# Two branches' first scores in one product, and sums of squares taken by ScalarE's accumulator

## The chip, the cores and the metric

The kernel runs on one core of one Trainium2 chip. The metric is the device time of one execution in microseconds, as the median of several runs: 623.28 us for the kernel before (three runs, 620.89 to 623.8). The engines are named as the profile names them: PE is TensorE (PEld its weight loads), DVE VectorE, ACT ScalarE, POOL GpSimd, SP SyncE.

## The reference, cut to what matters

The kernel computes a decoder trunk of two layers on 512 tokens of width 1024. Layer 0 has an mLSTM half and an attention half of 8 query heads in 2 groups, 64 wide. Attention has three branches; two of them, the selected blocks and the sliding window, come out here as plain causal attention, each with keys and values of its own.

```python
qh = partial_rope(rms_norm(heads(q, NSA_HEADS), q_norm), pos) * (d ** -0.5)
ks_h = partial_rope(rms_norm(heads(ks, G), k_norm[1]), pos)      # branch 0 in the kernel
kw_h = partial_rope(rms_norm(heads(kw, G), k_norm[2]), pos)      # branch 1
...
p_s = masked_softmax(s_s, tok_ok[:, :, None])
o_s = jnp.einsum('bgrqn,bgqnd->bgrqd', p_s, vs_g)
...
s_w = jnp.einsum('bgrqd,bgnd->bgrqn', q_blk, kwb)
...
return g_blk[..., 0:1] * o_c + g_blk[..., 1:2] * o_s + g_blk[..., 2:3] * o_w
```

`rms_norm` divides by the root of the mean square over the 64 elements of a head, so each q and k needs one sum of squares for every token and head: 8 for q, 4 for k (2 branches of 2 groups). Layer 1 is a gated linear recurrence, which the change leaves alone.

## The kernel before

All matrices of layer 0 are taken in groups of 512 columns (`Group`, `dense0`): cg, nq, nkv, nz, mq, mk, mv, mo, mz and the output projection. Each 512-column product exists three times, since weights and activations are split into a high and a low part in fp32r (`whi`, `wlo`, `h0h`, `h0l`). ScalarE makes `whi` and VectorE makes `wlo` from the loaded weights (`cvt_w`, L738), one group ahead.

Attention runs beside these products as strands of its own. For each of the four chunks of 128 tokens, `prep_q` (L1210) squares the 8 heads in one ScalarE instruction into a big buffer `sq`, lets GpSimd multiply q in place by the norm's weights, lets VectorE reduce `sq` to `qss`, lets GpSimd form the inverse root (`rsqrt_mean`, L710: a multiply-add and a power), and then VectorE scales (`x2`) and rotates. TensorE turns the result and ScalarE and VectorE drain it into high and low parts (`q2`). `prep_k` (L1239) does the same for the 4 key heads into `kd`. Both start when two of the five big buffers (`hb`, `b_t`, tag `big`) are free.

`nsa_a` (L1307) then goes through 16 units: 2 groups, 2 pairs, 2 branches, 2 halves (`UN`, L1303). For each of a unit's four chunks i it makes scores against keys up to that chunk, n = 128 (i + 1) columns, in two products (c = 0, 1) into a PSUM bank `sc` of which there are two. VectorE adds the mask and takes the row extreme (`nm`), ScalarE takes the exponential with its row sum (`sm`), and after the four chunks VectorE scales them by gate over sum. `nsa_b` turns the probabilities (`tp`), copies them (`PT`) and multiplies them with the values (`ac`).

The order of instructions on each engine isn't that of the source. `Flow` emits all operations of a layer under estimated times, and `Plan.flush` (L392) then lists them anew over the whole layer: `schedule` (L284) gives each engine its next operation by estimated start and latest due time, in six rounds of which the best is kept. The estimates for ScalarE and VectorE come from `price` (L517). For ScalarE it is this line, in which `scal` counts inputs of one column, an accumulator output among them:

```python
return low + (55 if psum else 93) + 95 * scal + (88 if "accum_out" in k else 0) + 0.833 * n - (95 if "accum_out" in k else 0)
```

So the engines run in a fixed order, each waiting for its next instruction only. All operations pass through one helper, so the profile gives L408 for nearly all of them; they are told apart by the tiles they write and read (out<-in).

Of the kernel before, what the change touches and what calls it, by code (L numbers as in the profile page):

```python
# [17 lines left out]
OP = mybir.AluOpType  # L18
# [597 lines left out]
def build(tc, I, out):  # L616
# [6 lines left out]
    with ExitStack() as ctx:  # L623
# [323 lines left out]
        with ExitStack() as c0:  # L947
# [261 lines left out]

            def prep_q(i):  # L1210
                yield hb(2)
                x = qk[i][:, :8, :]
                ts_ = slice(128 * i, 128 * (i + 1))
                sq = b_t("sq", (8, 64))
                A.activation(sq, x, AF.Square)
                P.tensor_tensor(x, x, cust(qnB, [[0, 8], [1, 64]]), op=OP.mult)
                ss = s_t("qss", [128, 8])
                V.tensor_reduce(ss, sq, axis=AX.X, op=OP.add)
                b_end()
                rq = s_t("qrs", [128, 8])  # L1220
                rsqrt_mean(rq, ss, 8, 1.0 / 64)
                x2 = b_t("x2", (8, 64))
                V.tensor_tensor(x2, x, cust(rq, [[1, 8], [0, 64]]), op=OP.mult)
                rot(x2, i)
                yield [None, TPS, (lambda: q2) if i else has(2)]
                if i == 0:
                    q2.extend(u_t("q2", (2, 2, 512), F32R) for _ in range(2))
                p4 = turn(x2)
                b_end()
                for o in range(2):  # L1230
                    a, b = slice(64 * o, 64 * o + 64), slice(64 - 64 * o, 128 - 64 * o)
                    for g in range(2):
                        pg = p4[a, 2 * g:2 * g + 2]
                        A.activation(q2[g][a, o, :, ts_], pg, AF.Copy)
                        V.tensor_tensor(q2[g][b, o, :, ts_], pg, q2[g][a, o, :, ts_].bitcast(F32), op=OP.subtract)
                fl.mark(E("q%d" % i))
                fl.add(cmp_sm(i), 2)

            def prep_k(i):  # L1239
                yield hb(2)  # L1240
                x = qk[i][:, 8:, :]
                ts_ = slice(128 * i, 128 * (i + 1))
                sq = b_t("sq", (4, 64))
                A.activation(sq, x, AF.Square)
                P.tensor_tensor(x.rearrange("p (a b) c -> p a b c", a=2), x.rearrange("p (a b) c -> p a b c", a=2),
                                cust(knB, [[64, 2], [0, 2], [1, 64]], 64), op=OP.mult)
                ss = s_t("kss4", [128, 4])
                V.tensor_reduce(ss, sq, axis=AX.X, op=OP.add)
                b_end()
# [57 lines left out]
            def nsa_a():  # L1307
                yield [E("q%d" % i) for i in range(4)] + [E("k%d" % i) for i in range(4)] + [E("gt")]
                for u, (g, pr, br, hh) in enumerate(UN):
# [3 lines left out]
                    nm = s_t("nm", [128, 4], 3)  # L1313
                    sm = s_t("sm", [128, 4], 3)
                    for i in range(NT):
# [3 lines left out]
                        for c in range(2):  # L1319
                            T.matmul(s[:, :n], q2[g][:, hh, pr, 128 * i:128 * (i + 1)], kd[g][:, c, br, :n],  # L1320
                                     start=c == 0, stop=c == 1)
                        V.tensor_tensor_reduce(s[:, :n], s[:, :n], cz[:, 512 - n:], 1.0, -NEG, op0=OP.add, op1=OP.min,
                                               accum_out=nm[:, i:i + 1])
                        A.activation(pp[:, OFF[i]:OFF[i] + n], s[:, :n], AF.Exp, bias=nm[:, i:i + 1], scale=-1.0,
                                     accum_out=sm[:, i:i + 1])
                    V.reciprocal(sm, sm)
                    V.tensor_tensor(sm, sm, cust(gt, [[24, 4]], 3 * hg + 1 + br), op=OP.mult)
                    for i in range(NT):
                        sl = slice(OFF[i], OFF[i] + 128 * (i + 1))
                        V.tensor_scalar(pp[:, sl], pp[:, sl], sm[:, i:i + 1], None, op0=OP.mult)  # L1330
                    PPs[u] = pp
# [6 lines left out]
            def nsa_b():  # L1338
                pts = []
                yp = None  # L1340
                for u, (g, pr, br, hh) in enumerate(UN):
                    yield [E("A%d" % u), hb(1)]
                    pp = PPs.pop(u)
                    ptl = b_t("PT", (1280,))
                    m = []
                    for kbs, o in (((0,), 0), ((1,), 512), ((2, 3), 896)):
# [3 lines left out]
                        for kb in kbs:  # L1350
                            for i in range(kb, NT):
                                T.transpose(tp[:, c:c + 128], pp[:, OFF[i] + 128 * kb:OFF[i] + 128 * (kb + 1)], idf)
# [766 lines left out]
```

## Time and profile before

| | |
|---|---|
| median of 3 runs | 623.28 us (620.89 to 623.8) |
| the profiled execution | 619.54 us |
| its span, first to last instruction | 617.8 us |
| mean granted clock of TensorE | 0.997 |
| TensorE busy | 609.2 us, 4498 products |
| VectorE busy | 463.9 us |
| ScalarE busy | 326.4 us |
| GpSimd busy | 104.5 us |

Rows of the trace all come from the one profiled execution. Its own time is 1.74 us over its span. Preparation of q and k lies at about 36 to 104 us of the span, the 16 units of attention at 104 to 235 us, the mLSTM heads and the output projection up to about 347 us, and layer 1 after that. A product's printed duration is longer than its distance to the next one, because products are pipelined and their ends are modelled; the distance between starts is what a product costs TensorE.

### The profile page before, as it was taken

The numbers are of one execution on the slowest core, as the hardware profiler recorded it, in microseconds if no ns is written. First come the engines' busy times: TensorE is split into PE (matmuls) and PEld (weight loads), VectorE is DVE, ScalarE is ACT, GpSimd is POOL, SyncE is SP. The second block draws the span as 40 slices with busy tenths as digits, with TensorE's granted clock in tenths as the row PEclk, the third lists the DMA queues.
The fourth block names the chain that finished last, engine by engine and source line by source line (L and its number), as shares of the span: only waits on it lengthen the run. The fifth ranks groups of instructions, "written<-read, shape, count | busy, mean of one in ns | idle before, by whom it ended". The sixth has DMA issues, their size and how long they took to land.

```text
span 617.8 us, 11670 instructions
## 1 busy us (share of the span) xinstructions
PE 609.2 (99%) x4498; PEld 492.0 (80%) x4498; DVE 463.9 (75%) x988; ACT 326.4 (53%) x778; POOL 104.5 (17%) x131
## 2 busy tenths in 40 slices
PE   8999998999999999999999999999999999999997
PEld 8877886877777777888888887788877877788886
DVE  5888989988899875656746669997688798986441
ACT  7554433675676765273534757447527375565410
POOL 1424252031100000063003111023000100122100
PEclk9998999999999999999999999999999999999999
DMA  8823137679994004016244424473222215473111
GB/s 293 278 117 103 51 103 256 203 164 342 247 203 138 0 2 147 7 46 228 77 162 136 154 85 138 118 240 121 69 72 69 70 34 173 138 282 128 35 69 68
DMA packets 23526, 82.90 MB, mean 134 GB/s; under 512 B 3376, under 2 KB 4272, under 8 KB 20656
## 3 DMA queue, kind: packets, MB, share of 16 engines
q1 hardware_dynamic: 21168, 65.39, 32.2%
q0 software_dynamic: 2304, 16.78, 10.3%
q8 instruction: 35, 0.57, 0.4%
q14 instruction: 19, 0.16, 0.1%
HBM read 77.96 MB, written 20.97 MB: 160 GB/s over the span
## 4 chain that ended last, share of the span: by engine, by line
PE 92%; DVE 3%; DMA 1%; issue 1%; POOL 1%; ACT 1%; SPq 0%; ACTq 0%; DVEq 0%
PE mm L408 35%; PE mx L408 17%; PE my L408 15%; PE sc L408 8%; PE tp L408 5%; PE ac L408 5%; PE tq L408 5%; PE sd L408 2%; DMA raw<-in_wall_dram 1%; DVE wlo L408 1%; DVE HB L408 0%; DVE AL L408 0%; POOL krs L408 0%; ACT whi L408 0%; DVE x L408 0%
## 5 line engine op out<-in xcount | busy, mean ns | idle before, releaser
L408 ACT ACTIVATE whi<-raw 128x512 fp32r<-128x512 f32 (+1 forms) x184 | 105.0, 614 | 76.2 <-PE my L408 29.5
L408 DVE TENSOR_TENSOR wlo<-raw,whi 128x1024 fp32r<-128x1024 f32 (+1 forms) x96 | 114.7, 1202 | 20.4 <-ACT whi L408 20.1
L408 PE MATMUL mm<-whi,h0h 128*128 128x512 f32 (+1 forms) x168 | 68.2, 407 | 0.0
L408 PE MATMUL mm<-whi,h0l 128*128 128x512 f32 (+1 forms) x168 | 67.9, 405 | 0.0
L408 PE MATMUL mm<-wlo,h0h 128*128 128x512 f32 (+1 forms) x168 | 67.4, 405 | 0.0
L408 ACT ACTIVATE PP<-sc,nm 128x128 f32<-128x128 f32 (+2 forms) x64 | 33.7, 527 | 26.0 <-DVE nm L408 22.9
L408 DVE CUSTOM_DVE_ANT_0 sc<-sc,cz 128x128 f32<-128x128 f32 (+2 forms) x64 | 31.4, 502 | 11.7 <-PE sc L408 9.1
L408 PE MATMUL mm<-h0h,whi 128*128 128x512 f32 x96 | 39.5, 411 | 0.0
L408 PE MATMUL mm<-h0h,wlo 128*128 128x512 f32 x96 | 38.1, 397 | 0.6 <-DVE wlo L408 0.6
L408 PE MATMUL mm<-h0l,whi 128*128 128x512 f32 x96 | 38.6, 402 | 0.0
L408 PEld LDWEIGHTS mm<-whi,h0l 128*128 128x128 f32 x168 | 32.1, 192 | 5.8 <-issue 0.2
L408 PEld LDWEIGHTS mm<-wlo,h0h 128*128 128x128 f32 x168 | 32.2, 192 | 5.6 <-issue 0.2
L408 PEld LDWEIGHTS mm<-whi,h0h 128*128 128x128 f32 x168 | 32.3, 192 | 5.2
L408 DVE TENSOR_TENSOR HB<-HB,tt 128x512 f32<-128x512 f32 x48 | 31.9, 687 | 4.4 <-PE sd L408 3.1
L408 PE MATMUL sc<-kd,q 128*128 128x512 f32 (+3 forms) x128 | 31.3, 330 | 0.0
L408 ACT ACTIVATE PT<-tp 128x384 f32<-128x384 f32 (+1 forms) x48 | 24.0, 526 | 9.5 <-PE tp L408 9.2
L408 POOL TENSOR_TENSOR ivgg<-ivgg,zz 128x256 f32<-128x256 f32 x16 | 17.8, 1116 | 65.9 <-ACT zz L408 65.9
L408 POOL TENSOR_SCALAR hr<-hs 128x4 f32<-128x4 f32 x12 | 2.3, 193 | 142.7 <-ACT hj L408 142.6
L408 PE MATMUL tp<-cs,PP 128*128 128x128 f32 x160 | 26.3, 275 | 0.0
L408 PEld LDWEIGHTS sc<-kd,q 128*128 128x128 f32 x128 | 22.7, 191 | 4.0 <-ACT PT L408 0.8
L408 PE MATMUL my<-h1l,whi 128*128 128x512 f32 x64 | 25.8, 403 | 0.0
L408 PE MATMUL mx<-h1l,whi 128*128 128x512 f32 x64 | 25.8, 402 | 0.0
(374 smaller groups left out, 1556.7 us busy)
## 6 DMA issues: line engine op xcount, KB each, us to landing
raw<-in_wall_dram SPq DMA_DIRECT2D x76, 512.0 KB, 3.8
wt<-in_wall_dram POOLq DMA_DIRECT2D x12, 1024.0 KB, 14.2
raw<-wt SPq DMA_DIRECT2D x16, 512.0 KB, 3.7
wt<-wt POOLq DMA_DIRECT2D x4, 1024.0 KB, 22.7
bias<-in_brow_dram SPq DMA_DIRECT2D x9, 256.0 KB, 4.1
xt<-in_xt_dram SPq DMA_DIRECT2D x8, 256.0 KB, 5.4
w<-in_cw_dram SPq DMA_DIRECT2D x2, 1024.0 KB, 9.4
x<-in_xt_dram SPq DMA_DIRECT2D x2, 1024.0 KB, 6.8
```

Source lines behind the costliest of these rows:

```text
L408: o.fn(*o.a, **k)
```

## The change

It has two parts. In `nsa_a`, a unit of branch 0 makes the scores of chunk 0 for both branches in one pair of products: the moving operand is `kd[g][:, c, :, :128]`, 2 x 128 columns, in place of the 128 of its own branch. The branch 1 half is masked and exponentiated at once into a small tile `e0`, and the unit of branch 1 with the same head starts at chunk 1; `nsa_b` turns chunk 0 from `e0` there. In `prep_q` and `prep_k`, each head is squared by an instruction of its own on ScalarE (`squares`), whose accumulator gives the sum; the reductions on VectorE and the big buffer for the squares are gone, and one free big buffer is asked for in place of two.

```diff
--- before.py
+++ after.py
@@ -1207,16 +1207,19 @@
                     T.transpose(p[:, 128 * c:128 * (c + 1)], flat(x2[:, 2 * c:2 * c + 2]), idf)
                 return cut(p, (4, 128))
 
+            def squares(x, ss):
+
+                j = cut(s_t("sqj", [128, 512], 1), (8, 64))
+                for a in range(x.shape[1]):
+                    A.activation(j[:, a, :], x[:, a, :], AF.Square, accum_out=ss[:, a:a + 1])
+
             def prep_q(i):
-                yield hb(2)
+                yield hb(1)
                 x = qk[i][:, :8, :]
                 ts_ = slice(128 * i, 128 * (i + 1))
-                sq = b_t("sq", (8, 64))
-                A.activation(sq, x, AF.Square)
+                ss = s_t("qss", [128, 8])
+                squares(x, ss)
                 P.tensor_tensor(x, x, cust(qnB, [[0, 8], [1, 64]]), op=OP.mult)
-                ss = s_t("qss", [128, 8])
-                V.tensor_reduce(ss, sq, axis=AX.X, op=OP.add)
-                b_end()
                 rq = s_t("qrs", [128, 8])
                 rsqrt_mean(rq, ss, 8, 1.0 / 64)
                 x2 = b_t("x2", (8, 64))
@@ -1237,16 +1240,13 @@
                 fl.add(cmp_sm(i), 2)
 
             def prep_k(i):
-                yield hb(2)
+                yield hb(1)
                 x = qk[i][:, 8:, :]
                 ts_ = slice(128 * i, 128 * (i + 1))
-                sq = b_t("sq", (4, 64))
-                A.activation(sq, x, AF.Square)
+                ss = s_t("kss4", [128, 4])
+                squares(x, ss)
                 P.tensor_tensor(x.rearrange("p (a b) c -> p a b c", a=2), x.rearrange("p (a b) c -> p a b c", a=2),
                                 cust(knB, [[64, 2], [0, 2], [1, 64]], 64), op=OP.mult)
-                ss = s_t("kss4", [128, 4])
-                V.tensor_reduce(ss, sq, axis=AX.X, op=OP.add)
-                b_end()
                 rk = s_t("krs4", [128, 4])
                 rsqrt_mean(rk, ss, 4, 1.0 / 64)
                 x2 = b_t("x2", (8, 64))
@@ -1305,30 +1305,38 @@
             ndone = [0]
 
             def nsa_a():
+                mm_, first = {}, {}
                 yield [E("q%d" % i) for i in range(4)] + [E("k%d" % i) for i in range(4)] + [E("gt")]
                 for u, (g, pr, br, hh) in enumerate(UN):
                     hg = 4 * g + 2 * pr + hh
                     yield [hb(1), lambda u=u: ndone[0] >= u - 1, SCS]
                     pp = b_t("PP", (1280,))
-                    nm = s_t("nm", [128, 4], 3)
-                    sm = s_t("sm", [128, 4], 3)
-                    for i in range(NT):
+                    if br == 0:
+                        for b_ in range(2):
+                            mm_[b_, hh] = s_t(f"nm{b_}", [128, 4], 3), s_t(f"sm{b_}", [128, 4], 3)
+                        first[hh] = s_t("e0", [128, 128], 3)
+                    nm, sm = mm_[br, hh]
+
+                    def chunk(s, n, i, p, nm, sm):
+                        V.tensor_tensor_reduce(s, s, cz[:, 512 - n:], 1.0, -NEG, op0=OP.add, op1=OP.min,
+                                               accum_out=nm[:, i:i + 1])
+                        A.activation(p, s, AF.Exp, bias=nm[:, i:i + 1], scale=-1.0, accum_out=sm[:, i:i + 1])
+                    for i in range(br, NT):
                         n = 128 * (i + 1)
                         yield SCS
                         s = sc_t()
                         for c in range(2):
-                            T.matmul(s[:, :n], q2[g][:, hh, pr, 128 * i:128 * (i + 1)], kd[g][:, c, br, :n],
-                                     start=c == 0, stop=c == 1)
-                        V.tensor_tensor_reduce(s[:, :n], s[:, :n], cz[:, 512 - n:], 1.0, -NEG, op0=OP.add, op1=OP.min,
-                                               accum_out=nm[:, i:i + 1])
-                        A.activation(pp[:, OFF[i]:OFF[i] + n], s[:, :n], AF.Exp, bias=nm[:, i:i + 1], scale=-1.0,
-                                     accum_out=sm[:, i:i + 1])
+                            T.matmul(s[:, :n] if i else cut(s, (2, 128)), q2[g][:, hh, pr, 128 * i:128 * (i + 1)],
+                                     kd[g][:, c, br, :n] if i else kd[g][:, c, :, :n], start=c == 0, stop=c == 1)
+                        chunk(s[:, :n], n, i, pp[:, OFF[i]:OFF[i] + n], nm, sm)
+                        if i == 0:
+                            chunk(s[:, 128:256], n, i, first[hh], *mm_[1, hh])
                     V.reciprocal(sm, sm)
                     V.tensor_tensor(sm, sm, cust(gt, [[24, 4]], 3 * hg + 1 + br), op=OP.mult)
                     for i in range(NT):
-                        sl = slice(OFF[i], OFF[i] + 128 * (i + 1))
-                        V.tensor_scalar(pp[:, sl], pp[:, sl], sm[:, i:i + 1], None, op0=OP.mult)
-                    PPs[u] = pp
+                        ps = pp[:, OFF[i]:OFF[i] + 128 * (i + 1)] if i or br == 0 else first[hh]
+                        V.tensor_scalar(ps, ps, sm[:, i:i + 1], None, op0=OP.mult)
+                    PPs[u] = pp, first[hh] if br else pp[:, :128]
                     fl.mark(E("A%d" % u))
                     if u % 8 == 7:
                         u_end(1 + u // 8)
@@ -1340,7 +1348,7 @@
                 yp = None
                 for u, (g, pr, br, hh) in enumerate(UN):
                     yield [E("A%d" % u), hb(1)]
-                    pp = PPs.pop(u)
+                    pp, p0 = PPs.pop(u)
                     ptl = b_t("PT", (1280,))
                     m = []
                     for kbs, o in (((0,), 0), ((1,), 512), ((2, 3), 896)):
@@ -1349,7 +1357,8 @@
                         c = 0
                         for kb in kbs:
                             for i in range(kb, NT):
-                                T.transpose(tp[:, c:c + 128], pp[:, OFF[i] + 128 * kb:OFF[i] + 128 * (kb + 1)], idf)
+                                src = pp[:, OFF[i] + 128 * kb:OFF[i] + 128 * (kb + 1)] if i else p0
+                                T.transpose(tp[:, c:c + 128], src, idf)
                                 c += 128
                         A.activation(ptl[:, o:o + c], tp[:, :c], AF.Copy)
                         m.append(fl.mark())
```

## Rows read from the trace of the kernel before

**Rows 1.** Busy table: busy us, share of span, instructions.

```profile
PE 609.2 (99%) x4498; PEld 492.0 (80%) x4498; DVE 463.9 (75%) x988; ACT 326.4 (53%) x778; POOL 104.5 (17%) x131
```

**Rows 2.** Chain that ended last, by engine.

```profile
PE 92%; DVE 3%; DMA 1%; issue 1%; POOL 1%; ACT 1%; SPq 0%; ACTq 0%; DVEq 0%
```

**Rows 3.** Stretches: length, busy us by engine (instructions), granted clock, DMA share, GB/s.

```profile
51.00:54.00 3.00, 3.00 (x8) 2.40 (x9) 2.78 (x6) 0.00 (x0) 0.00 (x0) 0.51 0.12 19
54.00:84.00 30.00, 30.00 (x155) 24.84 (x154) 27.17 (x58) 14.46 (x34) 14.14 (x14) 1.00 0.29 95
...
93.00:96.00 3.00, 1.20 (x5) 0.36 (x4) 2.93 (x8) 0.00 (x0) 1.50 (x3) 1.00 0.93 326
...
104.00:235.00 131.00, 131.00 (x731) 100.96 (x731) 110.67 (x316) 88.10 (x228) 11.40 (x16) 1.00 0.59 161
...
400.00:617.80 217.80, 213.23 (x2070) 173.21 (x2069) 157.17 (x305) 102.52 (x262) 28.41 (x36) 1.00 0.35 112
```

**Rows 4.** Timeline of PE: start us, us, engine, line, operation, out<-in, shapes.

```profile
110.65 0.33 PE L408 MATMUL sc<-kd,q 128*128 128x128 f32 x2
110.82 0.45 PE L408 MATMUL mm<-h0l,whi 128*128 128x512 f32 x1
111.11 0.39 PE L408 MATMUL mm<-h0h,wlo 128*128 128x512 f32 x1
111.34 0.39 PE L408 MATMUL mm<-h0h,whi 128*128 128x512 f32 x1
111.58 0.40 PE L408 MATMUL mm<-h0l,whi 128*128 128x512 f32 x1
111.81 0.40 PE L408 MATMUL sc<-kd,q 128*128 128x256 f32 x2
112.05 0.40 PE L408 MATMUL mm<-h0h,wlo 128*128 128x512 f32 x1
112.28 0.39 PE L408 MATMUL mm<-h0h,whi 128*128 128x512 f32 x1
```

**Rows 5.** Groups by line and shape, PE: count | busy us, mean ns | idle before.

```profile
L408 PE MATMUL sc<-kd,q 128*128 128x128 f32 x32 | 6.6, 267 | 0.0
```

**Rows 6.** The same view of DVE and ACT, 28 to 104 us.

```profile
L408 DVE TENSOR_REDUCE qss<-sq 128x8 f32<-128x512 f32 x4 | 2.7, 675 | 0.0
...
L408 DVE TENSOR_REDUCE kss<-sq 128x4 f32<-128x256 f32 x4 | 1.6, 412 | 0.1
...
L408 ACT ACTIVATE sq<-qk 128x512 f32<-128x512 f32 x4 | 2.5, 628 | 2.5 <-DVE qk L408 2.5
...
L408 ACT ACTIVATE sq<-qk 128x256 f32<-128x256 f32 x4 | 1.7, 416 | 3.6 <-DVE qk L408 3.5
```

**Rows 7.** Timeline of ACT, the square of kr with its sum.

```profile
47.65 0.26 ACT L408 ACTIVATE kn<-kr 64x64 f32<-64x64 f32 x1 [1.20 <-DVE kr L408]
47.82 0.19 ACT L408 ACTIVATION_READ_ACCUMULATOR kn<-kr 64x1 f32 x1
```

**Rows 8.** Timeline of PE; in brackets the idle time before, and what ended it.

```profile
94.05 0.50 PE L408 MATMUL mm<-h0h,wlo 128*128 128x512 f32 x1 [0.59 <-DVE wlo L408]
...
95.99 0.63 PE L408 MATMUL tp<-cs,x 128*128 128x128 f32 x4 [1.21 <-DVE kd L408]
```

**Rows 9.** Timeline of POOL and DVE, 88 to 94 us.

```profile
88.36 1.22 POOL L408 TENSOR_SCALAR krs<-kss 128x4 f32<-128x4 f32 x1 [6.25 <-DVE kss L408]
...
91.40 0.69 DVE L408 TENSOR_TENSOR x<-qk,krs 128x512 f32<-128x512 f32 x1 [1.48 <-POOL qk L408]
...
92.01 1.98 DVE L408 TENSOR_TENSOR wlo<-raw,whi 128x1024 fp32r<-128x1024 f32 x1
...
93.92 0.41 DVE L408 TENSOR_REDUCE kss<-sq 128x4 f32<-128x256 f32 x1
```

## Prediction, made before the changed kernel ran

> **What bounds the kernel now.** I read the page's busy table first: TensorE (PE) is busy 609.2 us of a span of 617.8, VectorE (DVE) three quarters, ScalarE (ACT) half [rows 1]. Then the chain of work that ended last: 92% of it is TensorE, 3% VectorE [rows 2]. So a microsecond comes off the end only if it comes off TensorE: fewer or shorter products, or less standing still. The table by stretches says where it stands still [rows 3]. Inside attention (104 to 235 us) it is busy 131.00 of 131.00 us, so there only a cheaper product helps. From 93 to 96 us, in the last part of the preparation of q and k, it is busy 1.20 of 3.00 us while VectorE is busy 2.93: TensorE waits for VectorE. From 51 to 54 us it is busy throughout, but the granted clock is 0.51, which is the lower of its two levels (1.2 against 2.4 GHz). In layer 1, 4.57 us of 217.80 are idle, in pieces that the change does not touch.
>
> **Part 1, the scores.** Before, each of the 16 units (head and branch) makes two products of 128 columns for its first chunk, 32 in all [rows 5]. After, the eight units of branch 0 make two products of 256 columns and the eight of branch 1 make none. So 32 narrow products leave and 16 wider ones come. What a product costs is the distance to the next start, not its printed duration, which overlaps its neighbours. A 512-column product is 0.23 us from the next: 111.11 to 111.34 [rows 4]. From the narrow pair at 110.65 to 111.11 there are 0.46 us, holding the pair and one 512-column product: the pair costs 0.46 - 0.23 = 0.23. From the 256-column pair at 111.81 to 112.28 there are 0.47 us with one 512-column product: that pair costs 0.24. Twice the columns cost 0.01 us more. Sixteen narrow pairs (3.68) leave and eight wide ones (1.92) come: 1.76 us less. As TensorE has no idle time in this stretch, all of it is on the path.
>
> The Trainium skill, "TensorE: Matmul & The Clock Gate", section "Back-to-back issue gap", speaks against this gain: at full clock the gap is the columns divided by 2.4 GHz plus 2.5 ns. By it a narrow product is about 56 ns and a wide one about 109, and my estimate of the whole saving would be 8 x (4 x 55.8 - 2 x 109.2) ns = 0.04 us. The trace agrees for the wide product (0.12) and not for the narrow one (0.115).
>
> The other engines do as many instructions in this stage as before: 64 mask-and-minimum operations, 64 exponentials, 64 scalings. Five chunks fall to a branch 0 unit and three to a branch 1 unit. The wide bank of scores is held until both its halves are exponentiated, but 56 banks pass through the two buffers in place of 64. I cost this at nothing: TensorE's cover is the dense products beside it, at 131.00 of 131.00 us. If that cover were gone, the second half's mask and exponential would stand before the next-but-one bank.
>
> **Part 2, the sums of squares, VectorE's side.** Eight reductions leave: 4 x 0.675 + 4 x 0.412 = 4.35 us [rows 6]. Most of that is hidden. What is on the path is the piece at 93 to 96 us. TensorE first waits 0.59 us for a weight's low part (wlo), then 1.21 us until VectorE has drained k [rows 8]. VectorE is late there because at 91.40 it has waited 1.48 us for GpSimd (POOL), then does wlo for 1.98 us, and then the last reduction, 0.41 us [rows 9]. GpSimd in turn had waited for the reduction before this, since the inverse root begins with its sum [rows 9]. With the reductions gone, the queue up to the drain is shorter by at least two of them, 0.82 us; at most the whole 0.59 + 1.21 = 1.80 us goes. Because VectorE's wait for GpSimd hangs on the same reductions, I take a value nearer the upper end, 1.5. Next late is then the same wlo, which is due in the same order anyway.
>
> **Part 2, ScalarE's side.** Four squares of 512 (0.628) and four of 256 (0.416) leave, 4.2 us [rows 6]. In come 4 x 8 + 4 x 4 = 48 squares of 64 columns, each with a read of the accumulator. The nearest row is the square of kr, also 64 columns wide, though on 64 partitions: it starts at 47.65, its read starts at 47.82 and lasts 0.19, so 0.36 from first to last; laid end to end the two are 0.26 + 0.19 = 0.45 [rows 7]. I take 0.40: 3.2 us for a q, 1.6 for a k, 19.2 in all (17.3 to 21.6), so 15 us more than before (13.1 to 17.4). ScalarE is busy 14.46 of 30 us from 54 to 84 us [rows 3], so there is room; I cost it at nothing because of that idle time. Queued behind a block of squares on ScalarE are the high parts of weights (whi), the drains of q and k and the small activations of compression. Without the cover each block costs up to its 3.2 or 1.6 us.
>
> Two more waits move. The in-place multiplication of q or k on GpSimd must follow the last square, where one square stood before it; behind it on GpSimd stand the inverse root, for which VectorE waits, and issues of the wt transfers. GpSimd is busy 14.14 of 30 us from 54 to 84, so a shift of two or three microseconds fits as long as the mean does not vanish into the wait of rows 9. And the sum no longer stands in VectorE's queue. The two nearly cancel: a q's sum comes 3.2 us after its squares begin, before it came after 0.63 plus VectorE's queue plus 0.675. The gate of the preparation falls from two free big buffers to one, as the square's buffer is gone; that only lets it start earlier.
>
> **The sum.** Products -1.76, idle of TensorE -1.5: -3.26 us. The profiled execution took 619.54 us, 617.8 of span and 1.74 around it; it becomes 616.3. That execution lies 3.74 us under the median of the runs, 623.28. I put the same difference on the median: 623.28 - 3.26 = 620.0.
>
> **Rivals.**
> (a) Only the products count. The order of the whole layer is planned anew by the code's own costs, and another wait comes up where the idle piece was: -1.76, 621.5. For it: a planned order with every engine near its limit finds new late spots. Against: VectorE has 4.35 us less in exactly this stage.
> (b) More goes. All 1.80 us of the idle piece, and the stretch at the low clock too: 3.00 us at 0.51 hold 1.5 us that full clock would not need [rows 3]. It comes after TensorE has run small products between large ones from 47 us on, and with sums that come sooner those could spread out. -1.76 - 1.80 - 1.5 = -5.06, 618.2. Against: the small products belong to the gates and to compression, which stay.
> (c) The price of a product goes by its columns, which stay the same in total; then only the idle goes: -1.5, 621.8. Against it stand the 0.23 and 0.24 us of rows 4. It is what the Trainium skill, "TensorE: Matmul & The Clock Gate", section "Back-to-back issue gap", would lead to.
> (d) Slower: ScalarE's queue. The code's planner prices a square of 64 with a sum at 93 + 95 + 88 - 95 + 0.833 x 64 = 234 ns; at 0.40 each is 0.166 us late, 1.33 us for a q and 0.66 for a k, 8.0 us in all that the order doesn't know of. If squares stand ahead of the whi and the drains for which TensorE is waiting, this lands on TensorE: +8.0 - 1.76 = +6.2, 629.5. It becomes slower by over 0.5% from 4.9 us landed on. For it: TensorE already stands in 93 to 96 us for work of this stage. Against: half of ScalarE is idle from 54 to 84.
> (e) Nothing: what the products give is eaten by waits of that kind, 1.8 us of them: 623.3.
>
> **How the numbers follow.** The measurement tells about 0.5% (3.1 us) from no change. Forecast 0.44, of which 0.30 lies beyond 3.1 us and 0.14 within, since its sum is just past that line; (a) 0.18, (b) 0.16, (c) 0.05, (d) 0.11, (e) 0.06. Faster 0.30 + 0.16 = 0.46; same 0.14 + 0.18 + 0.05 + 0.06 = 0.43; slower 0.11. The range reaches from a microsecond under (b), for pieces of layer 1's 4.57 idle us that may come or go, to just over (e): 617.2 to 624.0. Outside it lie (d) and a little of (b).
>
> **What would show it.** Right, step by step: 112 products of scores by tile, none of branch 1 with 128 columns in first place, and pairs of 256 columns at 0.24 us; TensorE busy nearly all of the 3 us around the last k; no reductions into qss and kss4; 48 pairs of square and accumulator read about 0.40 apart. Wrong: waits of TensorE or of wlo for ScalarE's whi between 36 and 104 us (d); an idle piece of the same size a few microseconds elsewhere (a, e); a low-clock stretch that is gone (b) or a second one. The prediction fails if the order of layer 1 changes by more than these terms.

## The result, and the profile after

The changed kernel takes 624.73 us (median of 18 runs; 17 of them lie between 623.67 and 627.23); the kernel before, run beside it, takes 619.96 us (18 runs). Three executions far longer than the others of their kernel (one of the changed kernel, 985.86 us, and below one of thin_after, 662.02, and one of after_late_price8, 1193.04) are in no ratio. The ratio is 1.0077, with an interval of 1.0063 to 1.0092: 4.8 us slower, where 3.3 us faster was forecast. (The 623.28 us on which the forecast was built is the median of three of those 18 runs of before.) The profiled execution of the changed kernel takes 625.76 us, 624.0 of it span, against 619.54 and 617.8.

From the page of the changed kernel, the busy table and the chain that ended last by engine, to be laid beside [rows 1, 2]:

```profile
PE 609.5 (98%) x4482; PEld 491.2 (79%) x4482; DVE 455.6 (73%) x980; ACT 332.2 (53%) x866; POOL 104.4 (17%) x131
PE 88%; DVE 5%; DMA 3%; issue 1%; ACT 1%; POOL 1%; SPq 0%; DVEq 0%; ACTq 0%; POOLq 0%
```

The operations are those that the change names: 16 products fewer, 8 operations fewer on VectorE, 88 more on ScalarE. TensorE is as long busy as before though it has less to do, and DMA's part of the chain has grown from 1% to 3%. Who TensorE waited for (total us, times, longest):

```profile
PE tp L408 <- ACT PT L408: 5.1, 1, 5.1
PE sc L408 <- ACT whi L408: 1.5, 1, 1.5
PE tq L408 <- ACT kT L408: 1.2, 1, 1.2
PE ac L408 <- POOL hm L408: 1.0, 1, 1.0
PE tp L408 <- DVE kd L408: 0.8, 1, 0.8
```

The two waits of [rows 8] are gone but for 0.8 us. New are one wait of 5.1 us for PT and one of 1.2 for kT. The stretches, with the columns of [rows 3], say where:

```profile
93.00:96.00 3.00, 3.00 (x14) 2.44 (x13) 2.96 (x9) 1.37 (x9) 1.29 (x3) 1.00 0.92 306
140.00:152.00 12.00, 6.92 (x36) 5.61 (x35) 7.35 (x17) 4.46 (x12) 1.62 (x2) 0.91 1.01 290
152.00:164.00 12.00, 12.00 (x51) 8.18 (x50) 7.67 (x20) 4.79 (x15) 1.65 (x2) 0.81 1.03 254
...
104.00:235.00 131.00, 125.92 (x678) 97.27 (x677) 103.87 (x299) 82.49 (x217) 12.76 (x18) 0.97 0.59 161
```

The idle piece at 93 to 96 us is filled, as forecast. But attention, where TensorE was busy 131.00 of 131.00 us, now has a stop of 5.1 us in it, and after the stop a low clock. The stop on TensorE, and ScalarE's timeline around it (start us, us, ..., in brackets the idle time before and what ended it):

```profile
145.31 0.99 PE L408 MATMUL sc<-kd,q 128*128 128x384 f32 x4
151.37 0.90 PE L408 MATMUL tp<-cs,PP 128*128 128x128 f32 x3 [5.08 <-ACT PT L408]
```

```profile
142.44 1.15 ACT L408 ACTIVATE whi<-raw 128x512 fp32r<-128x512 f32 x2
150.21 0.63 ACT L408 ACTIVATE whi<-raw 128x512 fp32r<-128x512 f32 x1 [6.61 <-DMA raw<-in_wall_dram]
150.74 0.96 ACT L408 ACTIVATE PT<-tp 128x512 f32<-128x512 f32 x2
```

TensorE waits for PT, the copy of turned probabilities. PT stands on ScalarE behind the conversion of a weight (whi), and that stands 6.61 us for its load. ScalarE takes its instructions in order, so everything behind the conversion is late with it. The same stretch of the kernel before:

```profile
141.10 1.15 ACT L408 ACTIVATE whi<-raw 128x512 fp32r<-128x512 f32 x2 [0.64 <-PE mm L408]
...
144.12 0.98 ACT L408 ACTIVATE PT<-tp 128x512 f32<-128x512 f32 x2 [1.41 <-PE tp L408]
...
146.48 1.15 ACT L408 ACTIVATE whi<-raw 128x512 fp32r<-128x512 f32 x2
...
150.74 1.15 ACT L408 ACTIVATE whi<-raw 128x512 fp32r<-128x512 f32 x2 [0.35 <-PE mm L408]
```

Here PT stands ahead of the last two conversions, and the last comes at 150.74. The loads themselves are slow in both. The time from issue to landing of the three loads that SP issues from 136 to 150 us, changed kernel first, then before:

```profile
DMA to landing us min/median/max: 11.0/13.6/17.9
```

```profile
DMA to landing us min/median/max: 9.6/12.2/14.1
```

In the changed kernel the first of them is issued at 139.13 and lands at 150.1 (139.13 + 11.0); in the kernel before it is issued at 141.08 and lands at 150.7. So the load comes at the same time; what differs is that ScalarE reaches its conversion at 143.6 in the one and at 150.7 in the other. Loads from 105 to 117 us land in 3.4 to 4.7 us. What makes those after 136 slow is in the same stretches: the DMA share is 1.01 and 1.03, as GpSimd's wt transfers (1 MB each) fill all DMA engines.

The low clock after the stop, two microseconds at a time:

```profile
149.00:151.00 2.00, 0.00 (x0) 0.00 (x0) 0.00 (x0) 0.80 (x2) 0.82 (x1) 0.70 1.07 256
151.00:153.00 2.00, 1.63 (x6) 1.44 (x7) 0.00 (x0) 2.00 (x5) 0.00 (x0) 0.50 0.98 248
153.00:155.00 2.00, 2.00 (x6) 1.58 (x5) 0.93 (x4) 2.00 (x6) 0.00 (x0) 0.50 1.09 264
155.00:157.00 2.00, 2.00 (x6) 0.92 (x6) 2.00 (x5) 0.05 (x1) 0.00 (x0) 0.59 0.98 240
157.00:159.00 2.00, 2.00 (x18) 1.01 (x14) 1.97 (x4) 0.00 (x0) 0.00 (x0) 1.00 1.05 258
```

0.50 is the lower level, 1.2 of 2.4 GHz. From 151.37 to 157 the work costs 1.63 x 0.50 + 2.00 x 0.50 + 2.00 x 0.41 = 2.6 us more than at full clock. So the one late load costs 5.1 + 2.6 = 7.7 us.

**The whole account.** Every kernel here has 1824 products of 512 columns into mm, mx and my, in the same number. I numbered them from 0 in order of their starts, and the first five columns give how much later (+) or earlier (-) the n-th one starts than in the execution of before. At the 60th, the 600th and the 1800th all kernels have the same work behind them, apart from the 16 products that the shared product saves, so between these columns the difference is what that stretch cost or gave. At the 90th and the 240th the small products are mixed in otherwise in some kernels (552 products of all kinds stand before the 240th in before, part1 and thin_before, 556 in the changed kernel, 558 in part2), so there only kernels with the same count can be compared. The last three columns split each execution's span: TensorE's idle time, what the low clock cost (busy time by what the granted clock lacks of 1), and the rest, its work at full clock.

| kernel | 60th (before: 42.7 us) | 90th (55.9) | 240th (100.1) | 600th (253.6) | 1800th (602.9) | idle | low clock | work |
|---|---|---|---|---|---|---|---|---|
| before | | | | | | 8.6 | 1.7 | 607.5 |
| changed | -0.15 | -0.89 | -0.63 | +4.82 | +6.22 | 14.4 | 4.3 | 605.2 |
| part1 | -0.14 | -1.64 | -0.36 | -1.26 | -0.41 | 11.4 | 0.0 | 605.9 |
| part2 | +0.27 | +0.70 | +2.38 | +8.01 | +9.75 | 14.5 | 6.5 | 606.6 |
| thin_before | +0.13 | +0.15 | +0.13 | +0.09 | +1.59 | 10.6 | 1.7 | 607.0 |
| thin_after_look | -0.10 | -2.36 | -2.13 | -4.38 | -2.00 | 11.6 | 0.0 | 604.2 |
| after_late_price | +0.11 | -2.20 | -1.97 | -2.01 | -0.77 | 11.6 | 0.0 | 605.4 |
| after_late_price8 | +0.55 | -1.76 | -1.53 | -2.35 | -1.49 | 9.9 | 0.0 | 606.4 |

For the changed kernel: +5.1 us for the stop, +2.6 for the low clock after it, +0.8 for all other idle time (1.2 more for kT, 0.6 more for whi at the start of the kernel, 1.0 less around k), and -2.3 of work. The sum is +6.2, the difference of the spans. By place it is +5.0 between the 60th and the 600th product and +1.4 in layer 1. The 1.7 us that before loses to the low clock lie at 51 to 54 us; an execution without them (0.0 in the column) is ahead by that much, and that isn't bound to the order of its instructions (last section).

### The profile page after: what moved, and what is told of

Read it like the earlier page. It is cut to its first block, busy times and chain, and to the rows that moved or that the text cites. A ratio compares the mean times of both kernels' runs of the same rounds, so it can differ in the third digit from the quotient of the medians.

```text
span 624.0 us, 11724 instructions
## 1 busy us (share of the span) xinstructions
PE 609.5 (98%) x4482; PEld 491.2 (79%) x4482; DVE 455.6 (73%) x980; ACT 332.2 (53%) x866; POOL 104.4 (17%) x131
## 4 chain that ended last, share of the span: by engine, by line
PE 88%; DVE 5%; DMA 3%; issue 1%; ACT 1%; POOL 1%; SPq 0%; DVEq 0%; ACTq 0%; POOLq 0%
PE mm L408 32%; PE mx L408 17%; PE my L408 14%; PE sc L408 7%; PE tp L408 5%; PE ac L408 5%; PE tq L408 5%; DMA raw<-in_wall_dram 2%; PE sd L408 2%; DVE wlo L408 1%; DMA xt<-in_xt_dram 1%; DVE HB L408 1%; DVE ivgg L408 1%; DVE AL L408 0%; POOL qk L408 0%
## 5 line engine op out<-in xcount | busy, mean ns | idle before, releaser
L408 ACT ACTIVATE PP<-sc,nm 128x256 f32<-128x256 f32 (+3 forms) x56 | 30.8, 551 | 28.2 <-DVE nm L408 27.3
L408 DVE CUSTOM_DVE_ANT_0 sc<-sc,cz 128x512 f32<-128x512 f32 (+3 forms) x64 | 31.1, 503 | 14.1 <-PE sc L408 11.4
L408 PE MATMUL mm<-h0h,wlo 128*128 128x512 f32 x96 | 39.5, 411 | 0.0
L408 PE MATMUL tp<-cs,PP 128*128 128x128 f32 x152 | 23.9, 276 | 5.1 <-ACT PT L408 5.1
L408 PE MATMUL sc<-kd,q 128*128 128x256 f32 (+2 forms) x112 | 28.4, 345 | 0.0
L408 PEld LDWEIGHTS tp<-cs,PP 128*128 128x128 f32 x152 | 19.0, 141 | 10.3 <-ACT PT L408 5.7
## 6 DMA issues: line engine op xcount, KB each, us to landing
wt<-in_wall_dram POOLq DMA_DIRECT2D x12, 1024.0 KB, 19.2
```

Of the source, the lines that this page charges most:

```text
L408: o.fn(*o.a, **k)
```

## Experiments

**1. Each part alone.** part1 takes only the shared product of the first chunk (`nsa_a`, `nsa_b`), part2 only the squares (`prep_q`, `prep_k`).

```diff
  part1, on the kernel before
-    T.matmul(s[:, :n], q2[g][...], kd[g][:, c, br, :n], ...)
+    T.matmul(s[:, :n] if i else cut(s, (2, 128)), q2[g][...],
+             kd[g][:, c, br, :n] if i else kd[g][:, c, :, :n], ...)
  part2, on the kernel before
-    A.activation(sq, x, AF.Square)
-    V.tensor_reduce(ss, sq, axis=AX.X, op=OP.add)
+    squares(x, ss)
```

> The shared product of the first chunk alone; squares and reductions as before. Theory T (transfer): the changed kernel loses its time at 146 to 151 us, where ScalarE stands at a weight's high part for a load that lands 11 us after its issue because GpSimd's transfers fill the DMA engines, and TensorE waits behind the drain (PT) queued after it. T prices the part itself at -1.76 us, 618.2, if this order meets no late load, and says that any loss over that is such a wait, to be seen as idle TensorE after ACT PT or whi. Theory S (squares): the loss comes from the 48 squares in ScalarE's queue, so this part alone gives 618.2 whatever the loads do. Theory C (columns): a product is priced by its columns, so 620.0.

> The sums of squares from ScalarE's accumulator alone; scores as before. S: all of the loss is here, 624.73 + 1.76 = 626.5, as waits of TensorE, whi or the drains for ScalarE between 36 and 104 us. T: the idle piece at 93 to 96 us goes, 1.5 us, 618.5, unless the new order meets a late load again, which would then be one wait of 4 to 6 us between 104 and 170 us and not many small ones before 104.

Measured: part1 619.78 us beside 620.0 for before (ratio 0.9998, 0.9987 to 1.0008); part2 626.22 (1.0088, 1.0054 to 1.0123; only four runs, 623.8 to 629.32, of which the slowest is the one profiled). The squares alone are about as slow as the whole change. But most of part2's loss isn't where squares are made, 36 to 104 us. There two waits of 1.1 us stand in place of the 1.8 of [rows 8], and the low clock at 50 to 57 us cost 1.7 more than in before. The stop of 3.3 us and the low clock behind it, 3.1, lie in attention. Its stop on TensorE, what ScalarE and VectorE do ahead of it, and the stretch:

```profile
160.28 0.80 PE L408 MATMUL sc<-kd,q 128*128 128x256 f32 x2 [3.30 <-ACT PP L408]
```

```profile
155.08 1.15 ACT L408 ACTIVATE whi<-raw 128x512 fp32r<-128x512 f32 x2 [6.39 <-DMA raw<-in_wall_dram]
```

```profile
156.26 1.23 DVE L408 TENSOR_TENSOR wlo<-raw,whi 128x1024 fp32r<-128x1024 f32 x1 [6.69 <-ACT whi L408]
```

```profile
152.00:164.00 12.00, 8.70 (x31) 6.46 (x30) 7.74 (x21) 5.51 (x12) 1.44 (x2) 0.82 1.02 250
```

It is the same picture on other instructions, with one queue more in it: ScalarE's conversion waits 6.39 us for a load; VectorE's low part of the same weight waits for the conversion, and the mask of the scores stands behind it; the exponential (PP) waits for that, and TensorE for the exponential. part1, with the same operations in attention as the changed kernel, has no such stop and no gain either. Its 619.78 is the number of Theory C, 1.6 above that of T and S. The table says where the gain went: 1.5 us of work less, and 2.8 us of idle time more, mainly 1.4 for kT in layer 1, 1.1 more for whi at the start of the kernel and 0.5 for q's drain at 76 us. Who TensorE waited for in part1:

```profile
PE sc L408 <- ACT whi L408: 2.0, 1, 2.0
PE tq L408 <- ACT kT L408: 1.4, 1, 1.4
PE tp L408 <- DVE kd L408: 1.2, 1, 1.2
...
PE mm L408 <- DVE wlo L408: 0.6, 1, 0.6
PE tp L408 <- DVE q L408: 0.5, 1, 0.5
```

The third row (kd) and the wlo row are the idle piece of [rows 8], which without the squares' part stays.

**2. The transfers thinned, the order kept.** Theory: the stop comes from a load that is late behind the wt transfers and stands ahead of PT on ScalarE. Rivals: the squares are dear in themselves, or the new order is dear whatever the loads do. The edit cuts each wt transfer from 2048 to 64 columns. Layer 1 then loads plain weights in place of the sums, which are left out; the orders of TensorE, VectorE and ScalarE stay the same to the last row, in both kernels.

```diff
-        self.plan.add("P", self.eng.dma_start, (out, src), k, 1000.0)
+        self.plan.add("P", self.eng.dma_start, (out[:, :64], src[:, :64]), k, 1000.0)
...
-                        return wt[q][:, 2048 * c + o:2048 * c + o + 1024]
+                        return wblock(f"r{2 * q}", c)[:, o:o + 1024]
```

> The changed kernel with the order of TensorE, VectorE and ScalarE unchanged, instruction for instruction, but GpSimd's wt transfers cut from 2048 to 64 columns; layer 1 loads plain weights in place of their sums, so its output is another. T: loads land 3 to 5 us after issue throughout, the stop of 5.1 us at 146 us and the low clock behind it (2.3 us) go: 617.4 or less, and 2 to 3 us under the kernel before. S and any theory in which the new order itself is dear: no change, about 624.7.

> The kernel before with the same cut of the wt transfers, order of the three engines unchanged; layer 1 loads plain weights in place of sums, so its output is another. T: ScalarE waited for no load here between 104 and 235 us, so at most 1 us goes: 619 to 620. If transfers cost this kernel as much as the changed one, it falls by several us too, and the difference between the two stays near 4.8.

> A second look at the changed kernel with wt transfers cut from 2048 to 64 columns (layer 1 then loads plain weights, so the sums of weights are left out), for its profile. Late load (theory T): span 615 to 616, granted clock 1.000, raw loads at 128 to 160 us landing in 3 to 5 us, no wait of TensorE over 1.5 us between 104 and 235 us, and TensorE's idle piece at 93 to 96 us gone. Rival: idle pieces of 3 us or more remain there and the gain lies in layer 1.

Measured: thin_after 616.79 us (the median of three runs, without the one of 662.02; 0.9951, 0.9931 to 0.9970), thin_before 619.67 (1.0003, 0.9986 to 1.0019); thin_after_look, the same kernel again, 617.57. With the same order of instructions the changed kernel is now 2.9 us below the kernel before, where with its full transfers it was 4.8 above. The changed order isn't dear by itself, and neither are its squares. From thin_after_look, the landing of the loads issued from 136 to 150 us, and the two stretches of the stop:

```profile
DMA to landing us min/median/max: 3.4/3.6/4.3
```

```profile
140.00:152.00 12.00, 12.00 (x64) 8.61 (x63) 11.26 (x24) 6.76 (x15) 0.00 (x0) 1.00 0.50 148
152.00:164.00 12.00, 12.00 (x69) 10.22 (x68) 9.76 (x36) 9.06 (x26) 0.00 (x0) 1.00 0.00 1
```

Landing falls from 11 to 18 us to 3.4 to 4.3, and stop and low clock are gone. At the 600th product this execution stands 9.2 us ahead of the changed kernel's: the 7.7 of the late load, and the 1.5 by which they differ already at the 90th, a low clock at 50 to 56 us (last section).

**3. The transfers spread.** The sixteen wt transfers are to come 15 us apart in place of 10.5.

```diff
-PS = 95000.0, 10500.0
+PS = 95000.0, 15000.0
```

> The changed kernel in full, but GpSimd's sixteen wt transfers are set 15 us apart in place of 10.5 (first at the same point), so that less of them falls into 128 to 176 us. TensorE's, ScalarE's and SP's orders are those of the changed kernel to the last instruction, VectorE's but for one weight operation in the mLSTM part. Late load (theory T): the raw loads issued at 135 to 155 us land in under 8 us in place of 11 to 18, the whi wait for a load at 150 us falls from 6.6 us to under 2, TensorE's stop of 5.1 us and the 12 us at clock 0.81 after it are gone: 616.5 to 619. The order itself is dear (rival): the stop or others like it stay, 623 to 626. Thinning helped only because there was less work in layer 1 and in the transfers (rival): no gain here, 623 to 626.

> The kernel before, with the same spreading of the wt transfers (15 us apart in place of 10.5) and its orders on TensorE, ScalarE and SP unchanged. Late load (theory T): here no conversion of weights stands ahead of a late load and TensorE has no stop, so nothing is to be won: 619 to 621, the same as before within 0.2%. If the transfers cost TensorE something in any order (rival), this gains as many microseconds as the changed kernel does, 3 or more: under 617.

Measured: after_spread 622.95 us (1.0047, 1.0033 to 1.0060), outside all that was expected of it; before_spread 620.04 (0.9999, 0.9987 to 1.0012). The edit didn't do what it says. GpSimd has the transfers in its queue behind a scaling (th) that waits for ScalarE (8.41 us at 114.98 us in the changed kernel), and here it issues eight in a row at 118.13 us; the DMA share from 128 to 164 us stays at 1.01 to 1.03. Only the last four went out of the way, past 270 us. So the run doesn't test what it was made for. Its profiled execution, 625.20 us, is the slowest of its nine, so the profile doesn't show why the median is lower than the changed kernel's. It shows the same stop, shorter, in the landing of the loads and in TensorE's timeline:

```profile
DMA to landing us min/median/max: 9.6/11.7/16.0
```

```profile
151.42 0.55 PE L408 MATMUL tp<-cs,PP 128*128 128x128 f32 x3 [3.70 <-ACT PT L408]
```

The first load is 9.6 us under way in place of 11.0, and the stop is 1.4 us shorter (3.70 against 5.08). But it doesn't land sooner: it is issued at 140.56 and lands at 150.17, against 139.13 and 150.12 in the changed kernel. What differs is that TensorE comes to the stop 1.4 us later, at 147.7 in place of 146.3. The landing sets the end of the stop in both, as the theory has it. before_spread stays where it was, but as its DMA engines were hardly relieved either, that says little; that the transfers cost the kernel before nothing is shown by thin_before.

**4. The loads priced as they are.** The planner reckons with 0.9 + 1.1 us and the bytes at 360 GB/s for a load, 3.5 us in all, where 11 to 18 pass. So it sets the conversion ahead of PT, in the belief that the weight is there. Four times the transfer term for loads emitted between 110 and 190 us, 8 in the last kernel:

```diff
+        slow = 4.0 if 110e3 < self.flow.pe < 190e3 else 1.0
-        self.plan.add("Q", self.eng.dma_start, (out, src), {"_ns": n * 4 / 360.0}, 475.0)
+        self.plan.add("Q", self.eng.dma_start, (out, src), {"_ns": n * 4 / 360.0 * slow}, 475.0)
```

> The changed kernel in full, with one number of the planner altered: a load that is emitted between 110 and 190 us is priced at 4 times its transfer term (5.8 us in place of 1.46, for what the trace shows to take 11 to 18 in all). The transfers themselves stay as they are. Late load (theory T): the planner sets the high parts of late loads behind PT on ScalarE, the stop shrinks from 5.1 us to under 1.5: 617 to 621. If the planner's price has no part in it (rival), the stop stays at 4 to 6 us: 623 to 626.

> The kernel before, with loads emitted between 110 and 190 us priced at 4 times their transfer term, as in after_late_price; nothing of the change. TensorE's order stays but for a handful of rows, on ScalarE one pair of high parts moves behind four other rows. Late load (theory T): before has no stop to lose, so 619.3 to 620.8, and the 618.29 of after_late_price is then what the change itself brings once its order fits the loads. If the price is a gain of its own (rival): 618 to 618.7, and the change brings nothing.

> The shared product of the first chunk alone, with the same price for loads between 110 and 190 us; TensorE's order stays that of part1 but for a handful of rows. It had no stop, so theory T gives it nothing: 619 to 620.3 against 619.78 without the price. If its product gain of 1.76 us was hidden by a late load (rival): 618 to 618.6.

> The squares alone, with the same price for loads between 110 and 190 us; TensorE's order stays that of part2 but for a handful of rows. Late load (theory T): the stop of 3.3 us at 157 us shrinks to under 1.5 and the low clock after it goes, 226.2 becomes: 626.2 less 3 to 6 us, 620 to 623; the waits of 1.1 us at 68 and at 101 us stay, so the 1.5 us forecast for the squares are not all won. If the squares themselves are dear (rival): 624 to 627.

> The changed kernel in full, with loads emitted between 110 and 190 us priced at 8 times their transfer term (11.7 us, about what the trace shows) in place of 4. More of the order changes than with 4 times. Late load (theory T): the stop of 1.8 us left at 155 us goes too, 616 to 618. If the remaining stop was another's (rival): 618 to 620.

| kernel | median us | ratio to before, interval |
|---|---|---|
| after_late_price | 618.29 | 0.9974, 0.9959 to 0.9990 |
| before_late_price | 621.74 | 1.0037, 1.0018 to 1.0056 |
| part1_late_price | 620.06 | 1.0003, 0.9986 to 1.0020 |
| part2_late_price | 621.74 | 1.0027, 1.0011 to 1.0042 |
| after_late_price8 | 618.32 | 0.9986, 0.9973 to 0.9999 |

One number in the planner takes 6.4 us off the changed kernel and makes it a little faster than the kernel before, by 0.26%. Of after_late_price, the landing of the loads of 136 to 150 us, ScalarE's timeline and the stretches:

```profile
DMA to landing us min/median/max: 12.3/14.7/19.0
```

```profile
143.13 0.98 ACT L408 ACTIVATE PT<-tp 128x512 f32<-128x512 f32 x2 [0.72 <-PE tp L408]
...
150.29 1.15 ACT L408 ACTIVATE whi<-raw 128x512 fp32r<-128x512 f32 x2 [3.13 <-DMA raw<-in_wall_dram]
```

```profile
140.00:152.00 12.00, 12.00 (x65) 8.72 (x64) 8.32 (x20) 6.86 (x15) 1.63 (x2) 1.00 1.02 263
152.00:164.00 12.00, 10.16 (x55) 8.26 (x54) 11.20 (x32) 6.76 (x21) 1.65 (x2) 1.00 1.04 255
```

The transfers are as they were and the loads as late as before (12.3 to 19.0 us). ScalarE still waits 3.13 us for one, but PT has gone ahead of it. Of the stop 1.84 us are left (under 1.5 was expected), behind an exponential, and the clock stays at 1.00. It is the same load: VectorE's low part waits 2.98 us for the late conversion, and the mask stands behind it. With 8 times the price this rest goes too, and nothing more is won: idle time falls by 1.8 us, but work rises by 1.1 in an order that differs elsewhere, and 618.32 lies above the 616 to 618 expected. part2 becomes 4.5 us faster by the same number, its stop gone; its waits of 1.1 us at 67 and at 100 us stay, and it is still slower than before, so the squares alone bring nothing. part1, which had no stop, gains nothing. The stops come and go as the theory says.

One run doesn't fit: before_late_price should have stayed at 620 and is 2 us slower, outside what was expected of it. Its profile has no stop. It is 0.5 us behind from the start and loses another 1.1 in layer 1, where its order is that of before. It rests on five runs, four of them at a mean granted clock of 0.991 to 0.996, where 10 of 24 runs of before were below 0.998. What slows it beyond that stays open; that the price is no gain in itself it shows all the same.

## Why the prediction was wrong, point by point

**What bounds the kernel, right but read too narrowly.** TensorE bounds it, and attention was read off as busy 131.00 of 131.00 us [rows 3]. That was taken as cover: "I cost this at nothing: TensorE's cover is the dense products beside it". A stretch without idle time shows that all waits in it were hidden in this order, not by how much. In the kernel before, the last conversion comes at 150.74 and its load lands at 150.7. The view that shows how thin the cover was, the time from issue to landing of the loads, wasn't read.

**The products, right at their place.** The pair of 256 columns costs 0.23 us, and no product of 128 columns is left (the tile's instructions with durations in ns, smallest, median and largest, and the timeline):

```profile
L408 PE MATMUL sc<-kd,q x112: 277/337/687, 99.0 to 227.6; 128*128 128x256 f32 x48, 128*128 128x384 f32 x32, 128*128 128x512 f32 x32
```

```profile
113.46 0.40 PE L408 MATMUL sc<-kd,q 128*128 128x256 f32 x2
113.69 0.40 PE L408 MATMUL mm<-h0h,whi 128*128 128x512 f32 x1
```

From each product's start to the next one's, the sc products take 22.2 us in all in before, 20.3 in part1 and 20.4 in thin_after_look, so 1.8 to 1.9 less, where -1.76 was forecast. All of TensorE's work at full clock fell by 1.5 in part1 and by 2.3 in the changed kernel, but by 0.9 in part2 too, where no product differs; so the whole can't tell the term to better than a microsecond. Rival (c), that columns alone count, falls as a sum: by it the 32 narrow products would have taken half of 119 ns each, 1.9 us, and they took 3.69 in before. It doesn't fall for each: single ones take 58 to 206 ns, by what stands beside them. The Trainium skill, "TensorE: Matmul & The Clock Gate", section "Back-to-back issue gap", gives the formula that the prediction took from it for an isolated product, and says that it comes out too low for small products in a stream with weight loads. The trace agrees, with 115 ns for a narrow one on average against 56. So the section doesn't speak against the gain, as the prediction had it.

**The idle piece, partly right.** It went, as forecast (1.80 us before). But a new wait of 0.8 us for kd came at 87.5 us, so of the 1.5 us about 1.0 was won.

**The squares, mis-sized to the dear side.** Forecast was 0.40 us for a square and its read. One after the other they are 0.24 apart:

```profile
37.40 0.24 ACT L408 ACTIVATE sqj<-qk 128x64 f32<-128x64 f32 x1
37.54 0.19 ACT L408 ACTIVATION_READ_ACCUMULATOR sqj<-qk 128x1 f32 x1
37.63 0.24 ACT L408 ACTIVATE sqj<-qk 128x64 f32<-128x64 f32 x1
```

48 of them are 11.5 us, not 19.2. The lone pair of [rows 7] was taken from its first start to its last end and end to end, which leaves out that the next square starts under the read. The Trainium skill, "ScalarE: Activation LUTs", section "What ACT_TABLE_LOAD costs", says that back-to-back activations overlap by about 93 ns; by it, if the read counts as one more activation, which the page doesn't say, my estimate would have been 0.24 + 0.19 - 2 x 0.093 = 0.24, and the trace agrees. So the planner's 234 ns were right, and rival (d) rested on a price that was wrong. That it came out slower, as (d) had it, is luck; its mechanism didn't come: TensorE waits for nothing of ScalarE's between 36 and 104 us, and what holds ScalarE's queue at 143 us is a load, not a square.

**The step that failed.** The sum carried each edit's cost at its own place and took the order around it as given; the waits of the new order on ScalarE were costed at nothing. The prediction noted for rival (a) that "another wait comes up where the idle piece was", since the order is planned anew, and let it eat the gain of 1.5 us there. What came was 7.7 us, in a stretch that had no idle time: the stop was paid twice, first as idle time and then as low clock. The transfers were thought of only as issues behind GpSimd's multiplication, costed at nothing; that loads are late while they run is in the trace of before, in rows that I didn't take.

**Layer 1.** Forecast was no change. 1.4 us were lost, 1.2 of them in a wait for kT at 561 us. Compared row by row, every engine's order in layer 1 is that of before. It isn't chance either: seven profiled kernels with the shared product (changed, after_spread, thin_after_look, after_late_price, after_late_price8, part1, part1_late_price) wait 0.9 to 2.0 us for kT there, and of the six without it five don't wait and part2_late_price 0.3. So the wait goes with that part, and the prediction's "pieces that the change does not touch" was wrong there. In part1, whose wait of 1.42 us is the same one, ScalarE's queue shows the same pattern in small: a conversion waits 2.29 us for a load, and kT stands behind it.

```profile
553.66 0.63 ACT L408 ACTIVATE whi<-raw 128x512 fp32r<-128x512 f32 x1 [2.29 <-DMA raw<-in_wall_dram]
...
555.14 0.87 ACT L408 ACTIVATE kT<-tq 128x384 f32<-128x384 f32 x2
```

In the kernel before, that conversion waits 0.75 us and TensorE none. The load takes 5.0 us in part1 and 3.4 in before; what it meets there, and how the shared product brings it about, wasn't tested.

**The range and the chances.** The terms on which the forecast stands, -1.76 and -1.5, came to about -1.8 and -1.0. The sum was off by what it didn't hold: +7.7 for the late load and +1.4 in layer 1; what is left of the +6.2, about -0.1, is small waits and work that the traces don't assign. The 623.28 us that it started from were 3.3 us too high as well: the profiled 619.54 was no lucky execution, the median of 18 runs is 619.96. From there the forecast would have been 616.7, and the miss is 8 us. So it is no near miss that 624.73 lies only 0.7 outside the range. With the order kept and the loads on time the forecast would have been near: thin_after lies 2.9 us under thin_before.

## What to carry to other kernels

Where a planner lists instructions anew, a change is not only its own edits: any conversion or copy can come to stand behind a load, and as ScalarE and VectorE take their queues in order here, everything behind it waits as well. Before costing an edit at nothing, read how late the loads land in each stretch where the DMA share is near 1, and how much time lies between landing and first use; that is the slack which a new order can lose. Where a planner prices its loads by bytes alone, price them as the trace shows them under traffic before judging a change: here this turned 0.8% slower into 0.3% faster.

## What the runs showed of the hardware

**Loads under traffic.** A load of 512 KB that lands in 3.4 to 4.7 us at 105 to 117 us of the changed kernel, where the DMA engines have room, took 11.0 to 17.9 while GpSimd's transfers filled them (share 1.01 to 1.04), and 3.4 to 4.3 at the same place when these were thinned. When it was issued hardly mattered: in the changed kernel, after_late_price, after_spread and before the first of these loads is issued at 139.1, 138.0, 140.6 and 141.1 us and lands at 150.1, 150.3, 150.2 and 150.7. The Trainium skill, "DMA: Bandwidth & Descriptors", section "Queues, rings and completion order", says that each DMA engine takes turns between the queues it has work for, packet by packet. By turns alone between two queues a load would lose some half of the bandwidth, and my estimate would be about twice the 3.4 us; the trace shows three to five times. From 136 to 150 us the two queues shared the changed kernel's DMA engines like this (packets, MB, share of their time; q0 is GpSimd's, q1 SP's):

```profile
q0 software_dynamic: 521, 3.79, 86.9%
q1 hardware_dynamic: 173, 0.64, 14.3%
```

So the loads, under way for 10.9 of these 14 us, had about a seventh of the time and not half. How many queues or packets stood ahead was not tested.

**The clock between 50 and 56 us.** In the kernel before the granted clock was low at 51 to 54 us [rows 3]. It isn't bound to the order of instructions. The changed kernel's execution has it; that of thin_after_look, with the same orders on TensorE, VectorE and ScalarE, has not:

```profile
50.00:52.00 2.00, 2.00 (x7) 1.53 (x8) 1.90 (x6) 0.59 (x3) 1.24 (x2) 0.71 0.81 254
52.00:54.00 2.00, 2.00 (x6) 1.52 (x6) 0.35 (x3) 0.00 (x0) 0.17 (x1) 0.50 0.75 227
```

```profile
50.00:52.00 2.00, 2.00 (x10) 1.54 (x10) 1.88 (x5) 0.66 (x3) 1.18 (x2) 1.00 0.81 233
52.00:54.00 2.00, 2.00 (x11) 1.60 (x10) 0.44 (x3) 0.53 (x1) 0.25 (x1) 1.00 0.73 201
```

It costs these two stretches (1 - 0.71) x 2 + (1 - 0.50) x 2 = 1.6 us. So the 1.5 us that rival (b) hoped to win there are first of all a difference between executions: of 24 runs of the kernel before, in the last group of runs, 14 had a mean clock of 0.999 or 1.00 and took 619.36 us in the median, 10 had 0.995 to 0.997 and took 620.87. What decides in which execution it comes is open. It doesn't make the gains above: at a mean clock of 0.999 or 1.00 alone, after_late_price takes 617.98 us (7 runs) where before takes 619.91 (12 runs).
